# An RWKV-7 inverse on four column groups of TensorE, and a later load of the scan's keys

## The chip, the cores and the metric

The kernel runs on one core of a Trainium2 chip. The metric is the device time of one execution in microseconds (us). The kernel before was timed three times; its median is 2175.63 us (2170.63 to 2177.81).

## What is computed

One layer of a hybrid encoder, on 1024 prompt tokens and 256 sample tokens with shared weights: a token mixer with a short convolution branch and a bidirectional RWKV-7 branch, then a gated ConvFFN, then a gated per-layer embedding. The part that matters here is the RWKV recurrence, run forward and backward in time for 8 heads of 64:

```python
def step(S, inp):
    r_t, w_t, kk_t, b_t, k_t, v_t = inp
    sa = jnp.einsum('bhvk,bhk->bhv', S, kk_t)
    S = (S * w_t[:, :, None, :] - sa[..., None] * b_t[:, :, None, :]
         + v_t[..., None] * k_t[:, :, None, :])
    return S, jnp.einsum('bhvk,bhk->bhv', S, r_t)
```

Everything else is matrix products, norms and elementwise work in float32: `u @ w_in`, `conv3`, `w_branch_a/b`, `w_out`, `w_up`, `w_down`, `w_ple`, `w_ple_gate`. The large products are done as three products of a high and a low part (`hi*hi + hi*lo + lo*hi`).

## The kernel before, in words

All 1280 tokens are kept transposed in SBUF (tile U). One program runs stage after stage: input norm and projections, the RWKV scan, branch products and output projection, FFN, embedding. Nearly every operation goes through one recording helper (`Pin`), which keeps program order on each engine; that is why the profile names nearly all work L204, and why a reader goes by the tiles' names.

**The scan stage** is the loop `for n in range(N)`, N = 20 steps: ten forward (d = 0, n = 0 to 9), ten backward (n = 10 to 19). A step treats 128 tokens as two chunks of 64 for all 8 heads. The recurrence inside a chunk is solved with the inverse of a triangular 64 x 64 matrix per head and chunk, u = 0 to 7 on each half of the partitions (`par`). The inverse is built from 32 x 32 blocks:

- `a_gram(n+2)` makes the matrices (tile g in PSUM); VectorE (V in the code, DVE in the profile) masks them into AT, LS and ZL; SyncE writes AT's diagonal blocks to DRAM (dA), `load_u` reads them back spread out (U<-dA), and `b_inv(n+2)` inverts all 32 x 32 blocks at once on GpSimd (POOL in the profile; tiles W, tm): 62 operations.
- A step later `b_out(n+1)` writes the blocks to DRAM (dW<-W, four DMAs), `b_back(n+1)` reads them into the matrix Mt (MT<-dW, four DMAs), and `b_d(n+1)` transposes two blocks on DVE (Dm<-MT, one for each `par`).
- At the start of the next step `b_x2` multiplies AT's off-diagonal block with Dm (PSUM g<-Dm,AT) and copies the result to SBUF (tile X2; the profile writes X<-g). `b_m21` multiplies that with the other diagonal block (g<-MT,X) and copies the result into Mt (MT<-g). Then `c_sa` uses Mt (p<-R,MT).

A step on TensorE (PE) is, in the program's order: `b_x2`, `c_p1` (p<-SV,LS), `a_t` (transposes, g<-cst,K, copied by ScalarE, ACT, into ZL<-g), `b_m21`, `c_keep` (ACT alone, Sc<-SV), `a_gram` first half (g<-LS,K), `c_sa` (y<-SV,LS and p<-R,MT), `a_gram` second half, `c_z`. After that the second chunk follows, with *fill* between: `gap(us)` issues a share of the projections that are still to do (mm<-U,wh and mm<-U,wl). A step's gaps add up to 18.6 of these shares, so the fill of a step is fixed. The fill brings DVE work along: `wl<-raw,wh` (splitting a weight), `cvp<-mm`, `cvy<-cvp` (the convolution) and, from n = 11 on, a group norm (cvp, cvy) with its loads.

The tiles of the PSUM pool `pg` (tag g) rotate over four banks; a step takes eight of them.

Loads and stores are issued in program order on SyncE (SP in the profile) or, for the gates' stores d_thc and d_thr, on ACT. Each DMA takes one of eight semaphores in turn, in the program's order over SP and ACT together, and before it is issued it waits until the DMA that had this semaphore before it, the eighth before it, has landed. `load_l(n+3)` loads the scan's decayed keys and queries (LS<-d_c twice, LS<-d_q once; LS has four buffers) for a step three ahead.

Of the kernel before, what the change touches and what calls it, by code (L numbers as in the profile page):

```python
# [5 lines left out]
F32 = mybir.dt.float32  # L6
# [6 lines left out]
D = 1024  # L13
# [46 lines left out]
class B:  # L60
# [5 lines left out]
    def sb(self, pool, shape, dt=F32, tag=None, bufs=None):  # L66
        kw = {} if bufs is None else dict(bufs=bufs)
        return pool.tile(shape, dt, name=tag, tag=tag, **kw)
# [57 lines left out]
def build(tc, I, O, dbg=None, upto=99):  # L126
    b = B(tc, I, O)
    nc = tc.nc
    sb = b.sb
    V, A, G, PE, SP = nc.vector, nc.scalar, nc.gpsimd, nc.tensor, nc.sync  # L130
# [21 lines left out]
    def pool(name, bufs=1, space=None, side=None, waits=None):  # L152
        kw = {}
        if waits is not None:
            kw["reuse_waits"] = waits
        if space is not None:
            kw["space"] = space
        if side is not None:
            kw["side"] = side
        cm = tc.tile_pool(name=name, bufs=bufs, **kw)  # L160
        p = cm.__enter__()
        open_pools[id(p)] = cm
        return p
# [43 lines left out]
    PE, V, A, G, SP = (Pin(e) for e in free)  # L207
# [647 lines left out]
    AT = {0: ("a", 0), 1: ("a", 1), 5: ("a", 2), 3: ("a", 3), 4: ("b", 0), 2: ("b", 1), 6: ("b", 2)}  # L855
# [100 lines left out]
    for i in range(NT):  # L956
# [15 lines left out]
        for j in range(2):  # L972
            ps = sb(pt, [128, 4, 128], F32, "tp")
# [12 lines left out]
        if i == 6:  # L986
            ps = sb(pt, [128, 4, 128], F32, "tp")
# [59 lines left out]
    pg = pool("pg", 4, PSUM, waits="tile")  # L1047
# [25 lines left out]
    def load_l(n):  # L1073
        if n < N:
            d, g = steps[n]
            c, q = (d_cq[nm, d][:, g * 128:(g + 1) * 128].rearrange("(h p) x -> p h x", p=128) for nm in "cq")
            L = [LS[n % 4][:, i].rearrange("p (h c) t -> p h (c t)", c=2) for i in range(3)]
            e = G if n == 0 else SP
            for par in range(2):
                e.dma_start(L[par][halves[par]], c[halves[par]])  # L1080
            e.dma_start(L[2], q)
# [18 lines left out]
    def a_gram(n, h):  # L1100
        d, g = steps[n]
        S = st[n]
        if h == 0:
            S["AT"] = sb(wk, [128, 8, 64], F32, "AT", 3)
            S["dA"] = dr.tile([32, 32, 32], F32, name="dA", tag="dA", bufs=2)
            S["W"] = sb(wk, [128, 8, 32], F32, "W", 2)
            SP.dma_start(S["W"], I["consts"][:, C_WI:C_N].rearrange("p (c j) -> p c j", c=8))
        K, L, Zl, AT = S["K"], LS[n % 4], ZL[n % 3], S["AT"]
        bc = lambda c: cst[:, c:c + 64].unsqueeze(1).broadcast_to((128, 4, 64))
        MS, MQ = bc(C_MS[d]), bc(C_MQ[d])  # L1110
        pss = [sb(pg, [128, 4, 128], F32, "g") for par in range(2)]
        us = slice(4 * h, 4 * h + 4)
        for u in range(4):
            for par in range(2):
                rw = halves[par]
                PE.matmul(pss[par][:, u, :], K[rw, 4 * h + u, :], L[rw, par::2 - par, 4 * h + u, :], start=True, stop=True)
        cc, qc = slice(0, 64), slice(64, 128)
        for par in range(2):
            rw, ow, co, qo, ps = halves[par], halves[1 - par], par * 64, (1 - par) * 64, pss[par]
            V.tensor_tensor(AT[rw, us], ps[rw, :, cc], MS[rw], ALU.mult)  # L1120
            V.tensor_tensor(L[ow, par, us], ps[ow, :, cc], MS[ow], ALU.mult)
            V.tensor_tensor(Zl[:, par, us, qo:qo + 64], ps[:, :, qc], MQ, ALU.mult)
            if h == 1:
                for hh in range(2):
                    q = par * 2 + hh
                    SP.dma_start(S["dA"][q * 8:q * 8 + 8].rearrange("u s t -> s u t"), AT[q * 32:q * 32 + 32, :, hh * 32:hh * 32 + 32])

    def a_t(n):
        if n < 3:
            ZL[n] = sb(wk, [128, 2, 8, 128], F32, f"ZL{n}")  # L1130
        K, Zl = st[n]["K"], ZL[n % 3]
        pss = [sb(pg, [128, 8, 64], F32, "g") for par in range(2)]
        for u in range(8):
            for par in range(2):
                PE.transpose(pss[par][:, u, :], K[halves[par], u, :], ident[halves[par], halves[par]])
        for par in range(2):
            A.copy(Zl[:, par, :, par * 64:par * 64 + 64], pss[par])
# [7 lines left out]
    def b_inv(n):  # L1145
        d, g = steps[n]
        S = st[n]
        Ut = S["U"]
        W = S["W"]
        for i in (range(31) if d == 0 else range(31, 0, -1)):  # L1150
            cs = slice(0, i // 4 + 1) if d == 0 else slice(i // 4, 8)
            js = slice(i + 1, 32) if d == 0 else slice(0, i)
            nc_, nj = cs.stop - cs.start, js.stop - js.start
            tm = sb(wk, [128, 8, 32], F32, "tm", 1)
            G.tensor_tensor(tm[:, cs, js], W[:, cs, i:i + 1].broadcast_to((128, nc_, nj)),
                            Ut[:, i:i + 1, js].broadcast_to((128, nc_, nj)), ALU.mult)
            G.tensor_tensor(W[:, cs, js], W[:, cs, js], tm[:, cs, js], ALU.add)

    def quads(d):
        b1, b2 = (0, 1) if d == 0 else (1, 0)  # L1160
        c1, c2 = slice(b1 * 32, b1 * 32 + 32), slice(b2 * 32, b2 * 32 + 32)
        r1 = [slice(par * 64 + b1 * 32, par * 64 + b1 * 32 + 32) for par in range(2)]
        r2 = [slice(par * 64 + b2 * 32, par * 64 + b2 * 32 + 32) for par in range(2)]
        return c1, c2, r1, r2
# [26 lines left out]
    def b_x2(n):  # L1191
        d, g = steps[n]
        S = st[n]
        c1, c2, r1, r2 = quads(d)
        ps = sb(pg, [128, 4, 128], F32, "g")[:, 0:2, :].rearrange("p a (b j) -> p (a b) j", j=32)
        X2 = S["X2"] = sb(wk, [128, 8, 32], F32, "X2", 1)
        for u in range(8):
            for par in range(2):
                PE.matmul(ps[r2[par], u, :], S["AT"][r1[par], u, c2], S["D"][r1[par], u, :], start=True, stop=True)
        for par in range(2):  # L1200
            A.copy(X2[r2[par]], ps[r2[par]])

    def b_m21(n):
        d, g = steps[n]
        S, Mt = st[n], MT[n % 2]
        c1, c2, r1, r2 = quads(d)
        ps = sb(pg, [128, 4, 128], F32, "g")[:, 0:2, :].rearrange("p a (b j) -> p (a b) j", j=32)
        for u in range(8):
            for par in range(2):
                PE.matmul(ps[r1[par], u, :], S["X2"][r2[par], u, :], Mt[r2[par], u, c2], start=True, stop=True)  # L1210
        for par in range(2):
            A.copy(Mt[r1[par], :, c2], ps[r1[par]])

    def chunks(n):
        return (0, 1) if steps[n][0] == 0 else (1, 0)
# [151 lines left out]
    def gap(us, g=0):  # L1367
        k = max(1, round(us / 0.8))
        for _ in range(k):
            fill.run(us * share / k)  # L1370
            if g:
                next(gn, None)

    for n in range(N):
        share = max(0.0, fill.left - TAIL) / (N - n) / 18.6
        nx, nx2 = n + 1 < N, n + 2 < N
        run_side()
        load_l(n + 3)
        if n == 4:
            gn_weights()  # L1380
        b_x2(n)
        c_p1(n, 0)
        if n >= 11:
            gn = group_norm(gl_g, gl_t)

        if nx2:
            a_t(n + 2)
        else:
            gap(0.8)
        b_m21(n)  # L1390
        c_keep(n, 0)
        if nx2:
            a_gram(n + 2, 0)
        else:
            gap(1.0)
        c_sa(n, 0)
        if nx2:
            a_gram(n + 2, 1)
        else:
            gap(1.0)  # L1400
        c_z(n, 0)
        if nx2:
            load_u(n + 2)
            b_inv(n + 2)
        if n >= 11:
            gn_load(gl_g, (2,))
        gap(3.2, 1)
        c_p1(n, 1)
        c_keep(n, 1)
        load_k(n + 3)  # L1410
        if nx:
            b_out(n + 1)
        gap(1.0, 1)
        c_sa(n, 1)
        if nx:
            b_back(n + 1)
        gap(1.5, 1)
        c_z(n, 1)
        fill.until(v_block + 1)
        if nx2:  # L1420
            load_v(n + 2)
        gap(5.5, 1)
        if nx:
            b_d(n + 1)
        gap(7.4, 1)
        for _ in gn:
            pass
        if n >= 10:
            gl_g = steps[n][1]
            gl_t = gn_load(gl_g, (0, 1, 3))  # L1430
# [279 lines left out]
    ps = sb(pmm, [128, 512], F32, "mm")  # L1710
# [176 lines left out]
    for g in range(NG - 1):  # L1887
# [3 lines left out]
        for i in range(NT):  # L1891
            down(g, i)
            if i in ((2, 5) if g else (5, 8)):
                n = 2 * g + 2 + (i > (2, 5)[g == 0])
# [180 lines left out]
```

## Time and profile before

| | us |
|---|---|
| median of 3 runs | 2175.63 |
| the profiled execution: its time | 2179.25 |
| its span | 2177.5 |
| scan stage, n = 0 to 9 (334.2 to 604.5 of the span) | 270.3, PE busy 268.96 |
| scan stage, n = 10 to 19 (604.5 to 887.4) | 282.9, PE busy 276.13 |

The busy time of an engine says little here, since PE is busy 97% of the span. What counts in the scan stage are the starts of PE's groups in a step, the few waits of PE that the profile names, and the order of what ACT, DVE and SP do just before and just after a step begins. A matmul's record lasts 0.19 to 0.4 us, while matmuls start far closer than that: how fast a group goes is read from its starts. Steps begin with the first g<-Dm,AT; step 2 starts at 388.62, step 7 at 524.45, step 13 at 687.59, step 14 at 718.26 us.

### The profile page before, as it was taken

The numbers are of one execution on the slowest core, as the hardware profiler recorded it, in microseconds if no ns is written. First come the engines' busy times: TensorE is split into PE (matmuls) and PEld (weight loads), VectorE is DVE, ScalarE is ACT, GpSimd is POOL, SyncE is SP. The second block draws the span as 40 slices with busy tenths as digits, with TensorE's granted clock in tenths as the row PEclk, the third lists the DMA queues.
The fourth block names the chain that finished last, engine by engine and source line by source line (L and its number), as shares of the span: only waits on it lengthen the run. The fifth ranks groups of instructions, "written<-read, shape, count | busy, mean of one in ns | idle before, by whom it ended". The sixth has DMA issues, their size and how long they took to land.

```text
span 2177.5 us, 40081 instructions
## 1 busy us (share of the span) xinstructions
PE 2122.6 (97%) x15929; PEld 1842.6 (85%) x15929; DVE 1342.9 (62%) x2198; ACT 886.7 (41%) x1529; POOL 522.7 (24%) x1378
## 2 busy tenths in 40 slices
PE   6999999999999999999999999999999999999998
PEld 5877798888887787887889999999999888887886
DVE  5467823444445664565577677677777765556565
ACT  5556513333344444422455544444444511113444
POOL 4000046777776774000000000000000011125000
PEclk9999999999999999999999999999999999999999
DMA  4336675555566674635247422112223332233121
GB/s 154 111 102 179 178 209 126 129 139 133 124 180 179 177 195 139 234 124 168 96 131 205 141 77 76 64 64 77 70 76 121 145 109 87 87 114 114 44 85 54
DMA packets 345877, 273.16 MB, mean 125 GB/s; under 512 B 135549, under 2 KB 306907, under 8 KB 345691
## 3 DMA queue, kind: packets, MB, share of 16 engines
q1 hardware_dynamic: 332859, 245.96, 38.4%
q10 hardware_dynamic: 9632, 13.11, 1.7%
q0 software_dynamic: 3200, 11.54, 1.5%
q8 instruction: 125, 2.05, 0.4%
q14 instruction: 61, 0.50, 0.1%
HBM read 187.18 MB, written 83.36 MB: 124 GB/s over the span
## 4 chain that ended last, share of the span: by engine, by line
PE 60%; DVE 5%; DMA 3%; POOL 2%; issue 1%; ACT 1%; SPq 1%; ACTq 0%; DVEq 0%; POOLq 0%
PE mm L204 24%; PE X L204 13%; PE Y L204 10%; PE g L204 6%; PE m L204 3%; PE p L204 2%; POOL W L204 1%; POOL tm L204 1%; SPq L204 1%; DVE wl L204 1%; DVE h L204 1%; PE y L204 1%; PE tp L204 0%; DMA dW<-W 0%; DVE aj L204 0%
## 5 line engine op out<-in xcount | busy, mean ns | idle before, releaser
L204 PE MATMUL mm<-U,wh 128*128 128x512 f32 (+1 forms) x1872 | 519.4, 365 | 2.8 <-ACT U L204 2.3
L204 PEld LDWEIGHTS mm<-U,wh 128*128 128x128 f32 x1872 | 324.1, 189 | 68.7 <-issue 11.8
L204 PE MATMUL mm<-U,wl 128*128 128x512 f32 (+1 forms) x936 | 336.0, 359 | 1.0 <-POOL wl L204 1.0
L204 POOL TENSOR_TENSOR tm<-W,U 128x60 f32<-128x60 f32 (+24 forms) x620 | 200.4, 323 | 111.4 <-DMA U<-dA 63.6
L204 POOL TENSOR_TENSOR W<-W,tm 128x60 f32<-128x60 f32 (+24 forms) x620 | 214.4, 346 | 48.6
L204 PEld LDWEIGHTS mm<-U,wl 128*128 128x128 f32 x936 | 176.8, 189 | 29.4 <-POOL wl L204 1.6
L204 DVE TENSOR_TENSOR f<-f,mm 128x512 f32<-128x512 f32 x200 | 136.4, 686 | 101.5 <-PE mm L204 100.4
L204 POOL TENSOR_TENSOR MG<-raw,MG 128x1024 fp32r<-128x1024 f32 x5 | 12.1, 2413 | 654.2 <-ACT MG L204 654.2
L204 PE MATMUL X<-B,wh 128*128 128x384 f32 (+1 forms) x936 | 158.5, 315 | 2.9 <-DVE MGb L204 2.9
L204 DVE SCALAR_TENSOR_TENSOR h<-MGb,fcol,h 128x255 f32<-128x255 f32 (+1 forms) x176 | 152.6, 880 | 14.1 <-ACT h L204 12.3
L204 ACT CAST wh<-raw 128x512 fp32r<-128x512 f32 (+1 forms) x141 | 113.8, 808 | 116.4 <-PE Y L204 41.6
L204 PE MATMUL mm<-MG,act 128*128 128x512 f32 x600 | 158.6, 391 | 0.7 <-DVE f L204 0.6
L204 PEld LDWEIGHTS X<-B,wh 128*128 128x128 f32 x936 | 144.3, 189 | 3.4 <-DVE MGb L204 3.4
L204 PE MATMUL X<-B,wl 128*128 128x384 f32 (+1 forms) x804 | 137.2, 315 | 3.1 <-DVE MGb L204 2.9
L204 PEld LDWEIGHTS mm<-MG,act 128*128 128x128 f32 x600 | 112.9, 189 | 24.8 <-DVE f L204 1.4
L204 PEld LDWEIGHTS X<-B,wl 128*128 128x128 f32 x804 | 123.7, 190 | 3.7 <-DVE MGb L204 3.1
L204 PE MATMUL mm<-wh,MG 128*128 128x512 f32 x400 | 126.3, 394 | 0.0
L204 PE MATMUL g<-WG,MG 128*128 128x512 f32 x480 | 112.8, 391 | 0.0
L204 PEld LDWEIGHTS g<-WG,MG 128*128 128x128 f32 x480 | 89.4, 188 | 18.3
L204 DVE TENSOR_TENSOR AT<-g,cst 64x256 f32<-64x256 f32 x80 | 33.6, 420 | 106.9 <-PE g L204 105.9
L204 DVE TENSOR_TENSOR wl<-raw,wh 128x1024 fp32r<-128x1024 f32 (+1 forms) x68 | 75.2, 1106 | 34.8 <-ACT wh L204 34.4
L204 PEld LDWEIGHTS mm<-wh,MG 128*128 128x128 f32 x400 | 74.8, 187 | 18.5
(503 smaller groups left out, 4178.7 us busy)
## 6 DMA issues: line engine op xcount, KB each, us to landing
raw<-in_w_up SPq DMA_DIRECT2D x53, 512.0 KB
raw<-in_w_in SPq DMA_DIRECT2D x39, 512.0 KB
d_act<-h SPq DMA_DIRECT2D x22, 640.0 KB
MGb<-d_act SPq DMA_DIRECT2D x20, 640.0 KB
raw<-in_w_down SPq DMA_DIRECT2D x22, 512.0 KB
d_bk<-o SPq DMA_DIRECT2D x32, 320.0 KB
U<-dA SPq DMA_DIRECT2D x80, 128.0 KB
K<-d_bk SPq DMA_DIRECT2D x19, 512.0 KB
```

The source lines that it names most:

```text
L204: return lambda *a, **k: tc.keep_in_program_order(f(*a, **k))
```

## The change

`b_x2` and `b_m21` put heads u = 0 to 3 on the column groups that they used so far, and u = 4 to 7 on the two other column groups, so that four 32 x 32 tiles of the array are named in turn. Half of each result then lies on other partitions of PSUM than where it is needed; ACT copies the first half, DVE copies the second one across partitions. The number of matmuls is the same. `b_m21` comes directly after `c_p1`, and `a_t` after `c_keep`. `load_l(n+3)` is issued after `b_inv(n+2)` instead of at the step's start. Two gaps are changed by 0.8 each with the same sum, which puts `b_d(n+1)` 0.8 shares later.

```diff
-        ps = sb(pg, [128, 4, 128], F32, "g")[:, 0:2, :].rearrange("p a (b j) -> p (a b) j", j=32)
+        ps = sb(pg, [128, 4, 128], F32, "g")[:, 0, :].rearrange("p (b j) -> p b j", j=32)
         X2 = S["X2"] = sb(wk, [128, 8, 32], F32, "X2", 1)
-        for u in range(8):
-            for par in range(2):
-                PE.matmul(ps[r2[par], u, :], S["AT"][r1[par], u, c2], S["D"][r1[par], u, :], start=True, stop=True)
+        for u in range(4):
+            for v, r in ((u, r2), (u + 4, r1)):
+                for par in range(2):
+                    PE.matmul(ps[r[par], u, :], S["AT"][r1[par], v, c2], S["D"][r1[par], v, :], start=True, stop=True)
         for par in range(2):
-            A.copy(X2[r2[par]], ps[r2[par]])
+            A.copy(X2[r2[par], 0:4], ps[r2[par]])
+            V.tensor_copy(X2[r2[par], 4:8], ps[r1[par]])
...
-        for u in range(8):
-            for par in range(2):
-                PE.matmul(ps[r1[par], u, :], S["X2"][r2[par], u, :], Mt[r2[par], u, c2], start=True, stop=True)
+        for u in range(4):
+            for v, r in ((u, r1), (u + 4, r2)):
+                for par in range(2):
+                    PE.matmul(ps[r[par], u, :], S["X2"][r2[par], v, :], Mt[r2[par], v, c2], start=True, stop=True)
         for par in range(2):
-            A.copy(Mt[r1[par], :, c2], ps[r1[par]])
+            A.copy(Mt[r1[par], 0:4, c2], ps[r1[par]])
+            V.tensor_copy(Mt[r1[par], 4:8, c2], ps[r2[par]])
...
         run_side()
-        load_l(n + 3)
         if n == 4:
             gn_weights()
         b_x2(n)
...
-        if nx2:
-            a_t(n + 2)
-        else:
-            gap(0.8)
         b_m21(n)
         c_keep(n, 0)
         if nx2:
+            a_t(n + 2)
             a_gram(n + 2, 0)
...
             b_inv(n + 2)
+        load_l(n + 3)
         if n >= 11:
             gn_load(gl_g, (2,))
-        gap(3.2, 1)
+        gap(4.0, 1)
...
         if nx:
             b_d(n + 1)
-        gap(7.4, 1)
+        gap(6.6, 1)
```

The program's order on PE at the start of step 7, before (g<-Dm,AT is `b_x2`, p<-SV,LS `c_p1`, g<-cst,K `a_t`, g<-MT,X `b_m21`, g<-LS,K `a_gram`):

```order
L204 MATMUL g<-Dm,AT 32x32 x16
L204 MATMUL p_6189<-SV,LS_2161 64x64 x8
L204 MATMUL g<-cst,K 128x64 x16
L204 MATMUL g<-MT_2163,X_6170 32x32 x16
L204 MATMUL g<-LS_2159,K 128x128 x8
```

And with the change:

```order
L204 MATMUL g<-Dm,AT 32x32 x16
L204 MATMUL p_6216<-SV,LS_2161 64x64 x8
L204 MATMUL g<-MT_2163,X_6195 32x32 x16
L204 MATMUL g<-cst,K 128x64 x16
L204 MATMUL g<-LS_2159,K 128x128 x8
```

The second product has moved ahead of the transposes: only `c_p1` now stands between it and the first one.

DVE from the end of step 6 to the masks of step 7's `a_gram` (AT<-g), before:

```order
L204 TENSOR_TENSOR cvp<-mm,cvp 128x512
L204 STREAM_TRANSPOSE Dm<-MT_2163 32x256 x2
L204 TENSOR_TENSOR cvp<-mm,cvp 128x256
L204 TENSOR_SCALAR cvy<-cvp,pcol 128x1282
L204 SCALAR_TENSOR_TENSOR cvy<-cvp,pcol,cvy 128x1282 x2
L204 TENSOR_TENSOR wl<-raw,wh 128x1024
L204 TENSOR_TENSOR cvy<-mm,cvy 128x512
L204 TENSOR_TENSOR AT<-g,cst 64x256
```

With the change:

```order
L204 TENSOR_TENSOR cvp<-mm,cvp 128x512
L204 TENSOR_TENSOR cvp<-mm,cvp 128x256
L204 TENSOR_SCALAR cvy<-cvp,pcol 128x1282
L204 STREAM_TRANSPOSE Dm<-MT_2163 32x256 x2
L204 SCALAR_TENSOR_TENSOR cvy<-cvp,pcol,cvy 128x1282 x2
L204 TENSOR_TENSOR wl<-raw,wh 128x1024
L204 TENSOR_TENSOR cvy<-mm,cvy 128x512
L204 COPY X_6195<-g 32x128 x2
L204 COPY MT_2163<-g 32x4x32 x2
L204 TENSOR_TENSOR AT<-g,cst 64x256
```

The transposes stand two operations later, and DVE's two pairs of copies stand behind all of the step's leftover work, where DVE's first duty for PE was AT<-g before.

SP from the end of step 5 to the transposes' input in step 6, before:

```order
L204 DMA LS_2159<-d_c_59 64x4x128 x2
L204 DMA LS_2159<-d_q_61 128x4x128
L204 DMA W<-in_consts 128x256
L204 DMA dA<-AT 32x8x32 x4
L204 DMA U<-dA 32x1024 x4
L204 DMA raw<-in_w_in 128x8x128
L204 DMA K<-d_bk_57 128x4x256
L204 DMA dW<-W 256x1x32 x4
L204 DMA MT_2163<-dW 32x8x32 x4
```

With the change:

```order
L204 DMA W<-in_consts 128x256
L204 DMA dA<-AT 32x8x32 x4
L204 DMA U<-dA 32x1024 x4
L204 DMA LS_2159<-d_c_59 64x4x128 x2
L204 DMA LS_2159<-d_q_61 128x4x128
L204 DMA raw<-in_w_in 128x8x128
L204 DMA K<-d_bk_57 128x4x256
L204 DMA dW<-W 256x1x32 x4
L204 DMA MT_2163<-dW 32x8x32 x4
```

The three LS loads stand no longer ahead of dA, but between U<-dA and dW<-W. In step 1 the weight load raw<-in_w_in stands ahead of K<-d_bk as well, where it followed dW<-W before.

More of the change, by code (lines that the diff above doesn't have):

```diff
@@ L1206, in b_m21 @@
         c1, c2, r1, r2 = quads(d)
-        ps = sb(pg, [128, 4, 128], F32, "g")[:, 0:2, :].rearrange("p a (b j) -> p (a b) j", j=32)
-        for u in range(8):
-            for par in range(2):
-                PE.matmul(ps[r1[par], u, :], S["X2"][r2[par], u, :], Mt[r2[par], u, c2], start=True, stop=True)
+        ps = sb(pg, [128, 4, 128], F32, "g")[:, 0, :].rearrange("p (b j) -> p b j", j=32)
+        for u in range(4):
+            for v, r in ((u, r1), (u + 4, r2)):
+                for par in range(2):
+                    PE.matmul(ps[r[par], u, :], S["X2"][r2[par], v, :], Mt[r2[par], v, c2], start=True, stop=True)
         for par in range(2):
-            A.copy(Mt[r1[par], :, c2], ps[r1[par]])
+            A.copy(Mt[r1[par], 0:4, c2], ps[r1[par]])
+            V.tensor_copy(Mt[r1[par], 4:8, c2], ps[r2[par]])
     def chunks(n):
```

## The prediction

> **What bounds the kernel now.** I read the page's list of engines first, then what PE waits for in the scan stage (334 to 890 us), then PE's order of time at the start of step 7, then the other engines' order of time around the same moment.
>
> ```profile
> PE 2122.6 (97%) x15929; PEld 1842.6 (85%) x15929; DVE 1342.9 (62%) x2198; ACT 886.7 (41%) x1529; POOL 522.7 (24%) x1378
> ...
> PE g L204 <- DVE Dm L204: 4.5, 5, 2.1
> PE p L204 <- ACT R L204: 1.9, 1, 1.9
> ```
>
> PE sets the end. In the scan stage it waits long for two things only: five times for D, 4.5 us together, and once for R, 1.9 us. So the change can gain in two ways: shorter prelude work on PE in each of the 20 steps, or these 6.4 us. It loses whenever PE waits for something new. PE at the start of step 7:
>
> ```profile
> 524.45 0.69 PE L204 MATMUL g<-Dm,AT 32*32 32x32 f32 x32
> 525.08 0.69 PE L204 MATMUL p<-SV,LS 128*64 128x64 f32 x16
> 525.69 0.71 PE L204 MATMUL g<-cst,K 64*128 64x64 f32 x16
> 526.34 0.69 PE L204 MATMUL g<-MT,X 32*32 32x32 f32 x32
> 526.96 1.27 PE L204 MATMUL g<-LS,K 64*128 64x128 f32 x16
> 528.27 0.23 PE L204 MATMUL y<-SV,LS 64*64 64x64 f32 x2
> 528.28 0.24 PE L204 MATMUL p<-R,MT 64*64 64x64 f32 x2
> 528.33 0.23 PE L204 MATMUL y<-SV,LS 64*64 64x64 f32 x2
> ...
> 528.81 1.16 PE L204 MATMUL g<-LS,K 64*128 64x128 f32 x16
> 529.90 0.69 PE L204 MATMUL p<-SV,ZL 128*64 128x64 f32 x16
> ```
>
> The groups follow each other without a hole. From the first X^2 start the second product starts at 1.89, the first a_gram at 2.51, the state products at 3.82, the second a_gram at 4.36, c_z at 5.45.
>
> **A, four column groups.** How fast a group starts comes from its length less the mean of one record:
>
> ```profile
> L204 PE MATMUL g<-Dm,AT 32*32 32x32 f32 x640 | 15.2, 195 | 4.5 <-DVE Dm L204 4.5
> L204 PE MATMUL p<-SV,LS 128*64 128x64 f32 x640 | 32.4, 231 | 0.8
> L204 ACT COPY X<-g 32x256 f32<-32x256 f32 x40 | 14.5, 363 | 97.2 <-PE g L204 94.1 <-PE p L204 2.5
> L204 DVE COPY pcol<-tp 128x46 f32<-128x46 f32 x1 | 0.2, 186 | 0.0
> L204 DVE COPY wl<-mm 128x512 f32<-128x512 f32 x2 | 1.4, 683 | 0.0
> ```
>
> X^2's last start is 0.69 - 0.195 = 0.495 after its first, so a pair on two tiles takes 0.495 / 15.5 = 0.032. p<-SV,LS, 64 columns on two tiles, takes (0.69 - 0.231) / 7.5 = 0.061 a pair. The state products name four tiles, two y and two p, and four of them start within 528.33 - 528.27 = 0.06. So on the row that is nearest, four tiles cost what two cost, and X^2 and M21 would each go from 0.50 to 0.26. That is 0.24 x 2 x 20 = 9.6 us of PE's time at most, and nothing if the tiles don't overlap. The Trainium skill, "TensorEngine Tiling (Array Packing)", Restrictions and Gotchas, speaks against the edit: different row tiles cannot access one PSUM bank at once, and all four tiles now write one bank. The trace doesn't agree so far, since two row groups write one tile of PSUM here at 0.032 a pair; by the page the 9.6 would be 0.
>
> **B, what of it reaches the path.** Before, p1 and a_t lay between X^2 and M21; now only p1 does, and M21 needs the copies of X^2. ACT before:
>
> ```profile
> 525.19 0.75 ACT L204 COPY X<-g 32x256 f32<-32x256 f32 x2 [5.98 <-PE g L204]
> 525.97 0.37 ACT L204 COPY R<-p 128x256 f32<-128x256 f32 x1
> 526.44 1.07 ACT L204 COPY ZL<-g 128x512 f32<-128x512 f32 x2
> 527.40 0.75 ACT L204 COPY MT<-g 32x256 f32<-32x256 f32 x2
> ```
>
> The first copy starts 0.74 after X^2's first matmul, 0.245 after its last one. With the last one at 0.26, copies can start at 0.505. ACT copies half the elements: its X and ZL rows (256 in 0.363, 512 in about 0.54) give 0.7 ns an element, so 128 take about 0.27, and two end at 1.05. DVE's two rows give (683 - 186) / (512 - 46) = 1.07 ns an element, so 128 take 0.27, and two end at 1.07 if DVE is free. p1 ends its starts at about 0.9, and M21 starts at 1.13, with a hole of 0.15. Its starts end at 1.39, and a_t, now behind it, takes 0.65 (525.69 to 526.34), so the first a_gram could start at 2.04; but its second bank is M21's, which MT's copies free at about 2.25, for 2.51 before. ACT now has R, MT, Sc ahead of ZL, and ZL's end (about 4.1) frees the bank that the second a_gram takes; it ended at 3.06 before and had slack. So c_z starts near 5.24 for 5.45: 0.2 a step of the possible 0.48, some 4 to 5 us in 20 steps. I take **-5**; ends 0 and -9.6.
>
> **C, DVE's copies stand in a queue.** DVE had no duty for PE before AT<-g, 3.7 after the step's start. DVE before, step 7, then step 2, then step 13:
>
> ```profile
> 519.85 0.44 DVE L204 STREAM_TRANSPOSE Dm<-MT 32x256 f32<-32x256 f32 x1 [0.57 <-DMA MT<-dW]
> ...
> 521.91 3.21 DVE L204 SCALAR_TENSOR_TENSOR cvy<-cvp,pcol,cvy 128x1282 f32<-128x1282 f32 x2
> 525.04 1.36 DVE L204 TENSOR_TENSOR wl<-raw,wh 128x1024 fp32r<-128x1024 f32 x1
> 526.33 0.68 DVE L204 TENSOR_TENSOR cvy<-mm,cvy 128x512 f32<-128x512 f32 x1
> 528.15 0.42 DVE L204 TENSOR_TENSOR AT<-g,cst 64x256 f32<-64x256 f32 x1 [1.14 <-PE g L204]
> ```
>
> ```profile
> 382.07 0.90 DVE L204 STREAM_TRANSPOSE Dm<-MT 32x256 f32<-32x256 f32 x2 [1.08 <-DMA MT<-dW]
> ...
> 387.94 1.33 DVE L204 TENSOR_TENSOR wl<-raw,wh 128x1024 fp32r<-128x1024 f32 x1
> ```
>
> ```profile
> 687.10 0.43 DVE L204 STREAM_TRANSPOSE Dm<-MT 32x256 f32<-32x256 f32 x1 [6.99 <-DMA MT<-dW]
> 688.38 0.44 DVE L204 STREAM_TRANSPOSE Dm<-MT 32x256 f32<-32x256 f32 x1 [0.84 <-DMA MT<-dW]
> ...
> 689.70 0.69 DVE L204 TENSOR_TENSOR cvy<-cvp,cvy 128x512 f32<-128x512 f32 x1
> 690.31 1.36 DVE L204 TENSOR_TENSOR wl<-raw,wh 128x1024 fp32r<-128x1024 f32 x1
> ```
>
> In step 7, 5.1 us of work (521.91 to 527.01) stand behind D and ahead of the copies, and end 2.56 after the step's start; AT hid that, it waited 1.14 more for PE. If D keeps its time the chain now ends between 0.95 (what stood between D and the chain has moved ahead of D, 1.6 us) and 2.56; if D is later by the LS loads, up to 3.1. Those loads cost SP this, and stand between U and dW now:
>
> ```profile
> 664.58 1.28 SPq L204 DMA_DIRECT2D LS<-d_c  x2
> 665.90 0.60 SPq L204 DMA_DIRECT2D LS<-d_q  x1
> ```
>
> So 1.9 us of issue. With copies at 2.6 and 0.55 for the pair, M21 starts at 3.2 in place of 1.13: I take a stall of 2.1 (0.4 to 2.6). In step 2 the work behind D ends at 389.27, 0.65 after the start at 388.62; raw and LS now stand ahead of K and dW in step 1, which puts D up to 3 us later, so 3.0 (0.2 to 3.2). In steps 12, 13 and 17 D lands at about the step's end, and cvy and wl, 0.69 + 1.36 = 2.0, stand behind it: about 1.2 each, 3.6. In the other steps DVE is idle at the start. Sum **+8.7**; ends 2 and 14. Behind the waiting copy on DVE stand MT's copies, AT and the masks, so the whole prelude is late, and no filling matmuls stand between X^2 and M21 to cover it.
>
> **D, the clock.** What a hole of this size does to PE's clock, in windows (length, busy time of PE, PEld, DVE, ACT, POOL, granted clock, DMA share, GB/s):
>
> ```profile
> 688.79:692.20 3.41, 3.32 (x71) 3.03 (x73) 2.81 (x4) 1.23 (x4) 3.10 (x5) 0.50 0.70 207
> 692.20:695.62 3.42, 3.42 (x72) 3.13 (x70) 0.54 (x2) 2.47 (x6) 2.71 (x10) 0.50 0.78 221
> 729.75:733.16 3.41, 1.48 (x36) 1.19 (x36) 2.24 (x4) 1.53 (x4) 2.80 (x8) 1.00 0.63 144
> 733.16:736.58 3.42, 3.42 (x35) 2.58 (x35) 0.37 (x1) 1.95 (x4) 0.68 (x4) 0.50 0.26 78
> ```
>
> The window with PE busy for 1.48 of 3.41 is followed by one at 0.50, in which half of 3.42 is lost, 1.7. A stall of 2 to 3 us leaves a window about as empty, if it falls into one. I charge two, steps 2 and 7: **+3.4**; ends 0 and 7. The Trainium skill, "TensorE: Matmul & The Clock Gate", Why this matters for your kernels, has the rate drop after idle gaps of over about 3 us. This trace's drop followed 1.9 us of idle in a window; by the page the 3.4 falls away.
>
> **E, what the change may remove.** R's wait in step 14 comes from ACT:
>
> ```profile
> 731.56 0.37 ACT L204 COPY R<-p 128x256 f32<-128x256 f32 x1 [3.80 <-DMA LS<-d_c]
> ```
>
> ACT stood at the issue of d_thc until the eighth DMA before it, an LS load issued late, had landed. With LS moved that eighth DMA is a load of cvp: 1.9 goes, and the half clock at 733.16 with it, 1.7; **-3.6**. Against D's 4.5 and the two slow windows from 688.79 (3.4): dA and U stand ahead of LS now and land 1.5 to 2 us earlier in steps 12 to 16, so POOL's inverse starts earlier; but dW stands behind LS, and its semaphore lanes fall on other DMAs. I take **-3** of these 7.9; ends -7 and +5.
>
> **Sum** on the profiled execution: -5 + 8.7 + 3.4 - 3.6 - 3 = +0.5, 2179.25 to 2179.8. It is 3.6 above the median of 2175.63 (runs 2170.63 to 2177.81), so carried to the median: **2176**, its own range 2170 to 2182.
>
> **The rivals.**
> 1. Faster, **2164**: D comes no later, since POOL's end and not SP sets dW, and the chains on DVE end inside 1 us. Then C is 2, D 0, B gives 7, E its 6.6: about -11.6. For it: PE's rows are packed, so shorter groups do move c_z; in steps 3 to 6 and 8 to 11 DVE is idle at the start. Against it: step 7's 5.1 us behind D.
> 2. Slower, **2187**: one mechanism, the LS loads in front of dW. From about 2 us of delay on, D is late for its step in 12 to 17, where it had none to spare (687.10 and 688.38 in step 13), and the copies stall behind it. C's 14 and E's +5 with D's 3.4, less 8.6 of B and R: about +14, less what the earlier U gives back, 2 to 3: +11. Against it: dA and U start earlier by what LS costs.
> 3. The four tiles don't overlap: they take turns at their one bank, and starts stay at 0.032 a pair. B becomes 0, the sum +5.5: **2181**. The state products' rows speak against it. The Trainium skill's page on array packing, Restrictions and Gotchas, is the rule for it.
>
> **How the numbers follow.** The forecast, no change that can be told, has 0.42; rival 1 0.32; rival 2 0.21; rival 3 0.05, half of it over the bound. A measurement of this kernel tells about 0.3% (6.5 us) from no change: 2169.1 to 2182.2. Faster 0.32; same 0.42 + 0.02 = 0.44; slower 0.24. The range reaches from 2161 to 2189, each rival's value with a few us of the unknown costs.
>
> **What would show it.** A: g<-Dm,AT groups of 0.45 for 0.69. B: c_z at about 5.2 after the step's start where nothing stalls. C: waits of PE for DVE's X in steps 2, 7, 12, 13 and 17, 1 to 3 us each, and none elsewhere. D: a clock of 0.50 behind those in steps 2 and 7. E: no wait for R in step 14; waits for D of less than 4.5. The prediction is wrong if no X wait is over 1 us (then rival 1), or if D is late for its step oftener than five times (rival 2).

## The result and the profile after

The change makes the kernel slower: 2210.86 us median of 5 runs (2205.44 to 2216.27) against 2172.76 (5 runs of before, 2169.54 to 2177.81), a ratio of 1.0174 with the interval 1.0157 to 1.0190. That is 38 us, far above the forecast of 2176 and outside the range of 2161 to 2189. The profiled execution took 2211.02 us, its span is 2209.2 with a mean granted clock of 0.985, for 0.993 before.

PE's waits in the scan stage (us in total, times, longest):

```profile
PE g L204 <- ACT X L204: 14.0, 18, 3.9
PE g L204 <- DVE Dm L204: 11.5, 10, 2.1
PE g L204 <- DVE MT L204: 2.8, 6, 0.5
```

Two of these lines are new, and the one for D has grown from 4.5 to 11.5. The wait for R is gone. (Two smaller lines follow, 2.3 for ACT's SV and 2.1 for "issue".) The first line names ACT, 18 times. What it means shows in a step in which nothing else goes wrong. PE, then ACT, then DVE at the start of step 6:

```profile
504.92 0.45 PE L204 MATMUL g<-Dm,AT 32*32 32x32 f32 x32
505.30 0.69 PE L204 MATMUL p<-SV,LS 128*64 128x64 f32 x16
505.91 0.24 PE L204 MATMUL g<-MT,X 32*32 32x32 f32 x2
506.36 0.76 PE L204 MATMUL g<-MT,X 32*32 32x32 f32 x30 [0.20 <-ACT X L204]
507.05 0.71 PE L204 MATMUL g<-cst,K 64*128 64x64 f32 x16
507.60 0.44 PE L204 MATMUL g<-LS,K 64*128 64x128 f32 x2
508.45 1.13 PE L204 MATMUL g<-LS,K 64*128 64x128 f32 x14 [0.42 <-issue]
...
510.13 1.16 PE L204 MATMUL g<-LS,K 64*128 64x128 f32 x16
511.22 0.69 PE L204 MATMUL p<-SV,ZL 128*64 128x64 f32 x16
```

```profile
505.44 0.26 ACT L204 COPY X<-g 32x128 f32<-32x128 f32 x1 [2.48 <-PE g L204]
506.05 0.26 ACT L204 COPY X<-g 32x128 f32<-32x128 f32 x1 [0.35 <-DVE X L204]
...
507.16 0.25 ACT L204 COPY MT<-g 32x128 f32<-32x128 f32 x1 [0.46 <-PE g L204]
507.76 0.26 ACT L204 COPY MT<-g 32x128 f32<-32x128 f32 x1 [0.35 <-DVE MT L204]
```

```profile
505.73 0.28 DVE L204 COPY X<-g 32x128 f32<-32x128 f32 x1 [4.08 <-ACT X L204]
506.34 0.29 DVE L204 COPY X<-g 32x128 f32<-32x128 f32 x1 [0.32 <-ACT X L204]
507.45 0.28 DVE L204 COPY MT<-g 32x128 f32<-32x128 f32 x1 [0.82 <-ACT MT L204]
508.05 0.30 DVE L204 COPY MT<-g 32x128 f32<-32x128 f32 x1 [0.32 <-ACT MT L204]
```

X^2 itself did what was expected, 0.45 for 0.69. But the four copies run one after another: ACT, DVE, ACT, DVE, each released by the one before on the other engine. They take from 505.44 to 506.63, where two engines side by side would be done in about 0.55. The same holds for MT's copies, 507.16 to 508.35, and the second of a_gram's two banks waits for the last of them (508.45). c_z starts 6.30 after the step's start, where it was 5.45.

In step 7 the same chain meets DVE's queue. PE, DVE, then the clock in windows (PE, PEld, DVE, ACT, POOL busy, granted clock, DMA share, GB/s):

```profile
533.29 0.24 PE L204 MATMUL g<-MT,X 32*32 32x32 f32 x2
537.17 0.95 PE L204 MATMUL g<-MT,X 32*32 32x32 f32 x30 [3.64 <-ACT X L204]
```

```profile
531.43 3.21 DVE L204 SCALAR_TENSOR_TENSOR cvy<-cvp,pcol,cvy 128x1282 f32<-128x1282 f32 x2
534.56 1.35 DVE L204 TENSOR_TENSOR wl<-raw,wh 128x1024 fp32r<-128x1024 f32 x1
535.83 0.68 DVE L204 TENSOR_TENSOR cvy<-mm,cvy 128x512 f32<-128x512 f32 x1
536.54 0.28 DVE L204 COPY X<-g 32x128 f32<-32x128 f32 x1
```

```profile
533.00:536.41 3.41, 0.53 (x15) 0.35 (x10) 3.33 (x3) 0.07 (x1) 3.18 (x4) 1.00 0.21 69
536.41:539.82 3.41, 2.65 (x51) 2.43 (x53) 1.25 (x5) 1.89 (x6) 2.71 (x10) 0.50 0.67 198
539.82:543.24 3.42, 3.42 (x52) 3.08 (x52) 2.05 (x6) 1.68 (x5) 2.71 (x10) 0.50 0.22 76
```

PE stands for 3.64 us, and the clock is at 0.50 for two windows after it. In the scan stage of the change there are seven such pairs of windows (in steps 2, 7, 11, 12, 13, 15 and 17), 47.8 us at half clock; before there were one pair and one single window, 10.2 us. Where PE has work throughout, the difference is up to 19 us of loss.

Step by step, from the starts of the first g<-Dm,AT: steps 2 and 7 are 5.7 us longer each; the other steps up to 9 are 0.06 to 0.9 longer, 3.7 together; steps 10 to 17 are 20.7 longer together. Step 18, which loses its gap of 0.8 with the change, is 1.6 shorter. The scan stage begins 0.7 earlier, and what follows the start of step 19 is 1.8 shorter. Together that is 31.7 us, the difference of the two profiled executions; the medians lie 38 apart, since the profiled execution of before (2179.25) took longer than each of its five runs here.

### The profile page after: what moved, and what is told of

It reads as the page before. It is cut to its first block, busy times and chain, and to the rows that moved or that the text cites. A ratio compares the mean times of both kernels' runs of the same rounds, so it can differ in the third digit from the quotient of the medians.

```text
span 2209.2 us, 40113 instructions
## 1 busy us (share of the span) xinstructions
PE 2128.8 (96%) x15929; PEld 1846.4 (84%) x15929; DVE 1366.2 (62%) x2278; ACT 879.5 (40%) x1529; POOL 513.3 (23%) x1378
## 3 DMA queue, kind: packets, MB, share of 16 engines
q1 hardware_dynamic: 332859, 245.96, 37.6%
## 4 chain that ended last, share of the span: by engine, by line
PE 64%; DVE 6%; DMA 4%; ACT 2%; issue 2%; SPq 1%; POOL 0%; ACTq 0%; DVEq 0%; POOLq 0%
PE mm L204 26%; PE X L204 13%; PE Y L204 10%; PE g L204 7%; PE m L204 3%; PE p L204 2%; PE y L204 1%; DVE wl L204 1%; DMA dW<-W 1%; SPq L204 1%; DMA MT<-dW 1%; PE tp L204 0%; DMA d_ob<-cvy 0%; DMA d_thc<-gth 0%; DVE cvy L204 0%
## 5 line engine op out<-in xcount | busy, mean ns | idle before, releaser
L204 POOL TENSOR_TENSOR W<-W,tm 128x60 f32<-128x60 f32 (+24 forms) x620 | 207.2, 334 | 48.6
L204 PEld LDWEIGHTS mm<-U,wl 128*128 128x128 f32 x936 | 176.7, 189 | 29.3 <-POOL wl L204 1.6
L204 PE MATMUL Y<-B,wh 128*128 128x384 f32 x420 | 85.2, 335 | 0.0
```

The costliest lines, as they stand in the source:

```text
L204: return lambda *a, **k: tc.keep_in_program_order(f(*a, **k))
```

## The experiments

Ratios are to the kernel before on the same chip, with their 95% intervals; 0.0100 is 22 us. The kernel before had 2171.7 to 2172.6 us in these comparisons. All kernels compute the whole reference.

### LS and the gaps put back

```diff
+        load_l(n + 3)
         if n == 4:
...
-        load_l(n + 3)
         if n >= 11:
             gn_load(gl_g, (2,))
-        gap(4.0, 1)
+        gap(3.2, 1)
...
-        gap(6.6, 1)
+        gap(7.4, 1)
```

> The change with the LS loads and the two gaps put back where they were. Theory (three separate costs: LS ahead of dW makes D late; the copies of X2 run one after another; DVE's queue in steps 2 and 7): the waits for D in steps 10 to 17 fall back from 11.5 to about 4.5 us and the half-clock windows there with them, so some 15 to 20 us below the change, 2190 to 2196; the X waits of steps 2 and 7 stay, shortened to 1 to 2.5 us. Rival (the longer prelude alone makes D late, since the loads of dA wait for it): D's waits stay near 10 us and the time within 6 us of the change, 2205 to 2214.

Measured: 2193.19, 1.0101 (1.0077 to 1.0124), 16 us below the change by the ratios, 18 by the medians. D's line in PE's waits falls from 11.5 to 0.8. Step 2 has no stall left, against the expectation; step 7 keeps one of 2.1. So the longer prelude alone does not make D late, and the rival falls. LS and the gaps went back together here; the runs below tell them apart. c_z stays at 6.31 in undisturbed steps: the serial copies have nothing to do with LS.

### LS and the gaps alone

```diff
-        load_l(n + 3)
         if n == 4:
...
             b_inv(n + 2)
+        load_l(n + 3)
...
-        gap(3.2, 1)
+        gap(4.0, 1)
...
-        gap(7.4, 1)
+        gap(6.6, 1)
```

> The kernel before with the LS loads moved behind the inverse and the two gaps changed, nothing else. Theory: D is late in 10 to 17, some 10 to 18 us over before, 2183 to 2191. Rival (the loads are harmless by themselves and only the longer prelude makes D late): within 5 us of before.

Measured: 2181.63, 1.0042 (1.0028 to 1.0055), 9 us above before, a little less than the 10 to 18 expected. The cost is there without the longer prelude. PE's waits for D are back, though c_z stands at 5.44 as before:

```profile
PE g L204 <- DVE Dm L204: 11.0, 11, 2.9
```

It came with something not looked for: steps 0 to 9 were 2.4 us shorter than before. That led to the runs on the gaps below.

### Two PSUM tiles for each product

```diff
-        ps = sb(pg, [128, 4, 128], F32, "g")[:, 0, :].rearrange(...)
+        pss = [sb(pg, [128, 4, 128], F32, "g")[:, 0, :].rearrange(...) for k in range(2)]
...
-                    PE.matmul(ps[r[par], u, :], ...)
+                    PE.matmul(pss[v // 4][r[par], u, :], ...)
...
-            A.copy(X2[r2[par], 0:4], ps[r2[par]])
-            V.tensor_copy(X2[r2[par], 4:8], ps[r1[par]])
+            A.copy(X2[r2[par], 0:4], pss[0][r2[par]])
+            V.tensor_copy(X2[r2[par], 4:8], pss[1][r1[par]])
```

(and the same in `b_m21`)

> The change with each of the two products written to two PSUM tiles, one read by ACT and one by DVE. Theory (the copies run one after another because both engines read one PSUM tile, which the program orders): ACT's and DVE's copies of a pair overlap, M21 starts its main part 1.1 to 1.2 us after the step's start instead of 1.44, c_z at 5.3 to 5.5 in place of 6.35 in unstalled steps, 0.45 to 0.9 us a step, 10 to 18 us below the change (2193 to 2201); the X waits of steps 2 and 7 stay at about 3.6. Rival (the engines contend for something else, such as the destination tile or a port): the copies still alternate and c_z stays at 6.3, the time within 4 us of the change.

Measured: 2190.36, 1.0083 (1.0068 to 1.0098), 20 us below the change, more than the 10 to 18 expected. Step 6 of this kernel, PE, ACT and DVE:

```profile
498.69 0.45 PE L204 MATMUL g<-Dm,AT 32*32 32x32 f32 x32
...
499.68 0.65 PE L204 MATMUL g<-MT,X 32*32 32x32 f32 x32
...
503.96 0.69 PE L204 MATMUL p<-SV,ZL 128*64 128x64 f32 x16
```

```profile
499.18 0.54 ACT L204 COPY X<-g 32x128 f32<-32x128 f32 x2 [2.43 <-PE g L204]
```

```profile
499.24 0.60 DVE L204 COPY X<-g 32x128 f32<-32x128 f32 x2 [2.81 <-PE g L204]
```

Now both engines wait for PE only and copy side by side, and c_z starts at 5.27. The copies alternated because the two engines read one PSUM tile, which the program orders with semaphores, tile by tile, even where they read other partitions; in the rows of the change each second copy is released by the other engine's. The destination tile was still shared in this run, so it is not the cause. The X waits of steps 2 and 7 stay (3.5 and 3.9), as they should.

### All copies on ACT

```diff
-            V.tensor_copy(X2[r2[par], 4:8], ps[r1[par]])
+            A.copy(X2[r2[par], 4:8], ps[r1[par]])
...
-            V.tensor_copy(Mt[r1[par], 4:8, c2], ps[r2[par]])
+            A.copy(Mt[r1[par], 4:8, c2], ps[r2[par]])
```

> The change with all eight copies on ACT and none on DVE. Theory (DVE's queue is what makes the 3.6 and 3.9 us X waits in steps 2 and 7): both go, with their half-clock windows, 10 to 12 us less; the copies of unstalled steps stay one after another, 4 x 0.27 on ACT, so c_z stays at 6.1 to 6.4: 2196 to 2202. Rival (those two steps wait for ACT or for PE's first product): the X waits of 2 and 7 stay over 2 us and the time near 2210.

Measured: 2193.70, 1.0093 (1.0075 to 1.0111), a gain of 17 us for the 10 to 12 expected. Steps 2 and 7 are 28.0 and 26.9 us long for 33.3 and 32.2 in the change, and have no stall, so DVE's queue is what made them. c_z stands at 6.30 as forecast; four copies on one engine (1.09) cost as much as the alternating ones. That is about 11 of the 17. In the same run D's waits are smaller, 8.5 us, the holes of 1.2 to 1.7 inside M21 in steps 12, 13 and 17 are gone, and the scan stage has 23.9 us at half clock for 47.8; how the rest of the gain divides among these is not shown.

### The gaps alone

```diff
-        gap(3.2, 1)
+        gap(4.0, 1)
...
-        gap(7.4, 1)
+        gap(6.6, 1)
```

> The kernel before with the two gaps of the change alone (3.2 to 4.0 and 7.4 to 6.6). In the run with the LS move and the gaps, steps 0 to 9 were 2.3 us shorter together, and the hole of 0.3 to 0.4 us ahead of the second p1, which waits for DVE's SV, was gone. Theory (the longer gap covers that wait, and the LS loads alone make D late): steps 0 to 9 some 2 to 3 us shorter, D's waits near the 4.5 us of before or 1 to 2 more, since D stands 0.8 share later: 2168 to 2173. Rival (the later D is what costs in steps 11 to 17): 2176 to 2182.

Measured: 2166.55, 0.9978 (0.9969 to 0.9988): faster than before by 5 us, and the best kernel of the study together with the next. Before, the second `c_p1` of step 6 stood with its weights, waiting for DVE's SV, and its matmuls took 1.04; PE's line of waits had not named it, because the wait lies on the weight loads (PEld) and is partly put down as "issue". PE and PEld of before:

```profile
506.67 0.40 PE L204 MATMUL mm<-U,wl 128*128 128x512 f32 x1
507.08 1.04 PE L204 MATMUL p<-SV,LS 128*64 128x64 f32 x16
```

```profile
507.05 0.19 PEld L204 LDWEIGHTS p<-SV,LS 128*64 128x64 f32 x2 [0.43 <-issue]
507.44 0.54 PEld L204 LDWEIGHTS p<-SV,LS 128*64 128x64 f32 x14 [0.20 <-DVE SV L204]
```

And PE with the gaps alone:

```profile
503.42 0.40 PE L204 MATMUL mm<-U,wl 128*128 128x512 f32 x1
503.75 0.69 PE L204 MATMUL p<-SV,LS 128*64 128x64 f32 x16
```

0.69 for 1.04; steps 0 to 9 take 266.3 us for 270.3. From the first to the last start of the second `c_p1`, ten of the 20 steps took 0.82 before, and nearly all take 0.46 now; over the 20 steps that is 5.2 us less, as much as the gain. The rival, that the later D costs, falls: D's waits are 2.0 in the profiled execution (2161.53 us).

### The gaps with D at its old place

```diff
-        gap(3.2, 1)
+        gap(4.0, 1)
...
-        gap(5.5, 1)
+        gap(4.7, 1)
```

> The kernel before with the gap ahead of the second p1 lengthened (3.2 to 4.0) and the one ahead of D shortened instead (5.5 to 4.7), so that D keeps its place. Theory: the hole ahead of the second p1 goes as in the run with both gaps, and D stands as before: 2167 to 2172, a few us under before. Rival (the second c_z or the loads behind it get worse by as much): within 2 us of before.

Measured: 2166.30, 0.9972 (0.9963 to 0.9982), no different from the gaps alone. Which of the two gaps the 0.8 is taken from does not matter; what matters is the 0.8 ahead of the second p1.

### LS behind dW

```diff
 (on top of the gaps alone)
-        load_l(n + 3)
         if n == 4:
...
             b_out(n + 1)
+        load_l(n + 3)
         gap(1.0, 1)
```

> The run of the gaps alone with the LS loads not at the step's start but right behind dW<-W. Theory (LS costs because it stands ahead of K and dW on SP, so dW lands 2 to 4 us later): with dW ahead of it D is in time, waits for D under 4 us in all, 2163 to 2171. Rival (it is enough that LS shares SP and the DMA engines with this part of the step, or that it no longer stands at the start): D waits of 8 us or more, 2176 to 2184.

Measured: 2170.91, 0.9995 (0.9983 to 1.0008), 10 us below the run with LS ahead of K and dW; the interval still touches that of the gaps alone. D's line shows 4.9, where less than 4 was expected. SP in step 11, first with LS ahead (the run of LS and the gaps alone), then with LS behind:

```profile
641.65 1.24 SPq L204 DMA_DIRECT2D LS<-d_c  x2
642.93 0.60 SPq L204 DMA_DIRECT2D LS<-d_q  x1
...
644.70 0.53 SPq L204 DMA_DIRECT2D K<-d_bk  x1
645.32 8.81 SPq L204 DMA_DIRECT2D dW<-W  x4
```

```profile
644.40 0.53 SPq L204 DMA_DIRECT2D K<-d_bk  x1
645.02 2.55 SPq L204 DMA_DIRECT2D dW<-W  x4
648.34 4.58 SPq L204 DMA_DIRECT2D LS<-d_c  x2
```

With LS ahead, SP stands 8.81 us in the issue of dW. SP's own waits over steps 10 to 17 of that run name d_thr, a store that must have landed before SP may reuse its semaphore:

```profile
SPq L204 <- DMA d_thr<-gth: 12.9, 3, 5.9
```

The longest of these, 5.9, lies in the stand of 8.81. With LS behind dW, SP waits for d_thr as much in all (13.7), but the 3.4 of them in step 11 fall on LS's issue, and dW is not held up. Over steps 10 to 17 the issue of dW's four DMAs takes 5.1 us on average with LS ahead, 5.1 in the change, 3.5 with LS behind, and 2.7 with the gaps alone.

In steps 10 to 17 dW has landed, on average, 23.2 us after the step's start before, 25.8 with LS and the gaps, 21.7 with LS behind dW, and 26.6 in the change. D needs the load that follows, MT<-dW, which has landed at 26.8, 29.3, 27.8 and 30.5, and at 26.3 with the gaps alone. PE's waits for D rise in the same order: 2.0 with the gaps alone, then 4.5, 4.9, 11.0 and 11.5. So LS costs because of what stands behind it on SP, and because it shifts which DMA waits for which landing. Behind dW it still stands ahead of MT<-dW, which fits D's waits not being down at 2.0; LS behind MT<-dW was not run.

### Both repairs

The change with two PSUM tiles for each product and `load_l` back at the step's start, as in the diffs above; the gaps stay at 4.0 and 6.6.

> The change with both repairs: two PSUM tiles for each product, and LS back at the step's start; the gaps stay as changed. Theory (the costs add up): 2210.9 - 20.5 - 17.7 = 2172.7, 2168 to 2177, with X waits of PE left in steps 7, 12, 13, 16 and 17 of 1 to 3 us each and no waits for D over 1 us. Rival (the two repairs take away the same loss, D's lateness by a long prelude): 2185 to 2190.

Measured: 2172.12, 1.0002 (0.9992 to 1.0012). The two repairs add up as the theory said: 18 more than two tiles alone, and D's line at 1.9. It is no faster than before, and 5 us slower than the gaps alone, though c_z is 0.17 earlier in undisturbed steps. Two waits remain. The first stands in the steps in which DVE has a queue (2, 7, 13 and 17 in PE's records); the second is as large, and 2.0 of it lie in step 19, with a window at half clock behind them (the last run comes back to it):

```profile
PE g L204 <- DVE X L204: 4.3, 4, 1.7
PE p L204 <- ACT SV L204: 4.4, 4, 2.0
```

### Both repairs, X2's copies on ACT where DVE is late

```diff
-            V.tensor_copy(X2[r2[par], 4:8], pss[1][r1[par]])
+            (A.copy if n in (2, 7, 12, 13, 16, 17) else V.tensor_copy)(X2[r2[par], 4:8], pss[1][r1[par]])
...
-        gap(5.5, 1)
+        gap(4.7, 1)
...
-        gap(6.6, 1)
+        gap(7.4, 1)
```

> As the last, but ACT makes all four copies of X2 in steps 2, 7, 12, 13, 16 and 17, in which DVE has a queue at the step's start, and D keeps its place (gap 5.5 to 4.7 instead of 7.4 to 6.6). Theory (what is left of the loss is DVE's queue): no X wait over 0.6 us, c_z at 5.3 in most steps, 2160 to 2168, below before. Rival (something else, such as D or the clock, still costs): 2170 or more.

Measured: 2174.84, 1.0012 (1.0001 to 1.0022), a miss. Of the X waits one of 0.6 is left, and the stall moved one group on: MT's second half is still DVE's, behind the same queue. In step 7 DVE reaches it at 525.34, 3.35 after the step's start, and PE waits 0.98 in the first a_gram for the bank that DVE then frees (at 525.95; the profile names ACT's ZL, which ends at about the same time):

```profile
525.34 0.61 DVE L204 COPY MT<-g 32x128 f32<-32x128 f32 x2
```

```profile
526.11 1.68 PE L204 MATMUL g<-LS,K 64*128 64x128 f32 x14 [0.98 <-ACT ZL L204]
```

### The order alone

```diff
 (on top of the gaps alone)
-        if nx2:
-            a_t(n + 2)
-        else:
-            gap(0.8)
         b_m21(n)
         c_keep(n, 0)
         if nx2:
+            a_t(n + 2)
             a_gram(n + 2, 0)
```

> The kernel before with the change's gaps (so to be compared with the run of the gaps alone, 2166.6) and M21 moved ahead of a_t, still on two column groups with ACT's copies. Theory (the order only pays with short copies): M21 waits for X2's copies till 1.53, a_gram's second bank for MT's copies till 3.05, and c_z falls from 5.45 to 5.9 to 6.0, +0.5 in 18 steps: 2173 to 2178. Rival (the order gains by itself, as p1 alone covers the copies): c_z at 5.2 to 5.4, 2162 to 2167.

Measured: 2175.72, 1.0020 (1.0009 to 1.0032), 9 us slower than the gaps alone; c_z at 6.10 in undisturbed steps, for 5.45. M21 ahead of a_t pays only with copies that are short: with the old ones it loses 0.65 a step, with two PSUM tiles and four column groups it wins 0.17.

### One more piece of the gap

```diff
 (on top of the gaps alone)
-        gap(1.5, 1)
+        gap(2.3, 1)
...
-        gap(6.6, 1)
+        gap(5.8, 1)
```

> The run of the gaps alone with one more piece of 0.8 moved from the last gap to the one ahead of the second c_z (1.5 to 2.3, 6.6 to 5.8), where PE's records show a hole of 0.2 to 0.4 us in some steps while ACT copies SV. Theory: those holes go, 1 to 4 us less, 2162 to 2166. Rival (D again 0.8 share later, with D at its step's end in 13 to 17): 2167 to 2172.

Measured: 2175.82, 1.0015 (1.0006 to 1.0024), 8 us slower than the gaps alone, beyond the rival's side. D's line is 4.3, so some of the room that D has is used up. The profiled execution also has a single wait of 3.4 for X in step 19, and 24 us at half clock in all. That wait is not D's: ACT, which copies X, had stood 5.4 us at the issue of its store d_thc until a weight load (raw<-in_w_in) had landed. How the 8 us divide between the two is not shown.

### The new form only where DVE is free

The repaired form of `b_x2`, `b_m21` and the order in twelve steps; steps 2, 7, 12, 13, 15, 16, 17 and 18 in the form of before; LS at its old place, the gaps of the change.

```diff
+QS = (2, 7, 12, 13, 15, 16, 17, 18)
...
+        q = n in QS
-        b_x2(n)
+        (b_x2_old if q else b_x2)(n)
```

> LS at its old place, the change's gaps, and four column groups with two PSUM tiles only in the steps in which DVE is free at the start; steps 2, 7, 12, 13, 15, 16, 17 and 18 as before. Theory (what is left of the loss with both repairs, 5.6 us against the gaps alone, is DVE's queue in these steps): c_z at 5.28 in 12 steps for 5.45 to 5.59, 2 to 3 us under the gaps alone, 2162 to 2166. Rival (the shorter prelude does not reach the end): 2166 to 2172.

Measured: 2171.64, 0.9997 (0.9986 to 1.0008), the rival's side: c_z is at 5.28 in the steps with the new form, but the kernel is 4 us slower than the gaps alone. The prelude gains 0.17 in twelve steps, 2 us, and the time does not show it. PE's waits in this run name ACT's SV (4.5 us in 3 times, the longest 3.2, in step 19). ACT ahead of that wait:

```profile
854.52 0.33 ACTq L205 DMA_DIRECT2D d_thc<-gth  x1
854.89 0.74 ACT L205 COPY SV<-p 64x256 f32<-64x256 f32 x2 [3.39 <-DMA raw<-in_w_in]
```

ACT stands at the issue of d_thc until a weight load has landed, as it did for R in step 14 of before, where the load was one of LS; a window at half clock follows. The same stand is in step 19 of both repairs (2.2 us), of the run with X2's copies on ACT where DVE is late (1.8), of the order alone (2.0), and of the one with one more piece of the gap (5.4), and not in that of the gaps alone. So part of what keeps these kernels behind the gaps alone is neither the prelude nor DVE's queue but this store. Whether the short prelude brings it about is open, and so is whether other executions than the profiled ones have it.

## Why the prediction was wrong

The account of the 1.74% by runs: the gaps -0.22 (gaps alone); LS +0.81 (two tiles, less both repairs); the alternating copies +0.91 (the change, less two tiles); the rest, +0.24 (both repairs, less the gaps alone), is what four column groups and the order win with copies side by side, set against what DVE's queue and the stand in step 19 cost. Together 1.74; it adds up by construction, since each kernel is compared with the next. Without the short copies and the new order LS costs less, 0.64 (LS and the gaps, less the gaps alone). By the forecast's own steps:

**A, right.** Four tiles cost what two cost: a group of X^2 takes 0.45 for 0.69, which is the 0.26 to the last start, as worked out, and the record's own 0.19. The Trainium skill, "TensorEngine Tiling (Array Packing)", Restrictions and Gotchas, keeps different row tiles from one PSUM bank at the same time; the trace differs, since here tiles of two row groups write one bank at this rate, and the third rival fell.

**B, the step that failed first.** It let ACT and DVE copy side by side, M21 starting at 1.13 and c_z at 5.24, and took -5. In the change M21's main part starts at 1.44 and c_z at 6.35 in undisturbed steps. With two PSUM tiles the forecast's own picture came true within 0.04, 5.28. (One row was misread, without consequence: a ZL copy takes 0.589 us by itself, not half of a group of two that overlap, so 128 elements on ACT come to 0.25, not 0.27; measured are 0.26.) So the sum of durations was right and a dependence was missing: two engines that read one PSUM tile take turns in this program. It cost 20 us, where a gain of 5 stood in the sum. The forecast had treated copies from one tile as free of each other, without a row that showed it. The Trainium skill has a warning that I did not weigh: "PSUM — Partial Sum Buffer", PSUM bank collisions raise a hardware error, has software keep any two engines apart that touch the same bank in the same 32 partitions, reads included. Here the two engines read different 32 partitions of one bank, which that rule would allow; the program orders whole tiles. No run here let them read one bank at once.

**C, mechanism right, sizes too small for two steps.** Steps 2 and 7 stall by 3.9 and 3.64 us; forecast were 3.0 and 2.1. What the sizes lacked is mostly the delay of D by LS: from two tiles alone to both repairs, where only LS moves, the two stalls fall from 3.5 and 3.9 to 1.7 and 0.7. All copies on ACT removes both. In steps 12, 13 and 17 the holes inside M21 are 1.5, 1.2 and 1.7, where 1.2 each was forecast.

**D, mis-sized.** It charged one window at half clock for each of two stalls. The clock stayed at 0.50 for two windows after each (6.83 us), and there were seven such stretches in the scan stage, not two, since late D's make holes as well. Forecast +3.4; the half-clock time rose by 37.6 us, up to 19 us of loss. The Trainium skill's figure for the gap, about 3 us ("TensorE: Matmul & The Clock Gate", Why this matters for your kernels), differs from these rows too: the window ahead of the stretch in step 13 had PE busy for 2.07 of 3.41, so idle for 1.3 us. Idle time in a window does not decide it by itself, though: a window of the same kernel with as much, in step 16, was followed by one at full clock:

```profile
710.47:713.88 3.41, 2.07 (x43) 1.34 (x43) 1.45 (x3) 0.03 (x1) 2.83 (x8) 1.00 0.54 101
829.94:833.35 3.41, 2.04 (x10) 1.26 (x8) 0.43 (x1) 0.60 (x1) 2.70 (x10) 1.00 0.41 106
```

**E, half right, and wrong where it weighed most.** R's wait went, as traced through the eighth DMA before d_thc: PE's waits of the change have no line for it. For D it expected -3 because dA and U start earlier; D's waits rose by 7, to ten in number, which is the sign that the forecast had named for its second rival (oftener than five times). U does land earlier in the run of LS and the gaps, 17.3 us after the step's start for 18.6, on average over steps 11 to 16, but dW lands 2.6 us later over steps 10 to 17: 1.9 us of LS, a later K, and a stand at the store d_thr. That is the mechanism of the second rival, with 0.21 and a price of +11. It was the right one for this part; measured by itself it is 14 us (LS and the gaps, less the gaps alone), and with the alternating copies on top it was not enough for the 38.

**What no step held.** The gap of 4.0 for 3.2 was told in the change and not costed. It is worth -5 by itself, on a wait of PE's weight loads that the forecast's view of waits (PE alone) does not list.

The forecast's chances gave 0.24 to slower. What made its range too narrow was not the sizes that it named as unknown but a dependence that it did not see, and losses that it took one by one though they feed each other: a late copy or a late D makes a hole, and a hole makes two slow windows.

## What to carry to other kernels

When work is split over two engines, look first for what the two share: here one PSUM tile made two short copies into a chain of four, and a second tile gave 20 us back. Read the waits of the weight loads beside those of PE, and take "issue" there as a question, for the only gain in this change (5 us) lay there. A load that is moved on a queue costs what stands behind it, and moves who waits for whose landing; put it behind the last transfer that someone waits for (here MT<-dW, which no run tried). Look at the stores that a computing engine issues, too: its next copy waits behind them.

## What the hardware showed that was not expected

The seven windows ahead of the change's slow stretches had PE busy for between 0.53 and 2.07 of 3.41 us, and all seven stretches lasted 6.83 us. Before, a window with 0.38 was followed by 6.83 and one with 1.48 by 3.42 only. Idle time alone does not tell which windows are followed by half clock (2.04 busy in step 16 was not), and what decides between one window and two stays open; in step 11 PE was busy throughout the first slow window (3.42 of 3.42) and the second came all the same:

```profile
645.61:649.02 3.41, 1.07 (x9) 0.47 (x7) 0.88 (x2) 0.00 (x0) 2.71 (x10) 1.00 0.70 160
649.02:652.44 3.42, 3.42 (x95) 3.05 (x95) 0.86 (x3) 1.36 (x5) 2.72 (x10) 0.50 0.83 235
652.44:655.85 3.41, 3.41 (x52) 3.14 (x49) 1.52 (x4) 1.92 (x5) 2.63 (x11) 0.50 0.54 153
```

ACT and DVE copy 128 elements across partitions in 0.26 and 0.28 to 0.30 us, and side by side from two PSUM tiles neither is slower (0.54 and 0.60 for two).
